# A hybrid decoder layer: the opening products on an input that has adaLN's scale but not yet its shift

## The chip, the cores and the metric

The kernel runs on one core of a Trainium2 chip. The metric is the device time of one execution in microseconds, the median of the runs. PE is TensorE (matmuls), DVE VectorE, ACT ScalarE, POOL GpSimd; SP issues the loads. Each engine works through its own instructions in order.

## The reference

One layer with hidden size D = 2048, T = 512 tokens, batch 1, all in float32:

```
mod = silu(c) @ w_ada + b_ada                  # shift, scale, gate: 2048 each
h = rms_norm(x, norm_w) * (1 + scale) + shift
proj = h @ w_in                                # aq ak av ag | q k v of DeltaNet | z | b a | mg_a mg_b
y_a = (sliding-window attention of aq, ak, av with sinks) * silu(ag) @ w_o_swa
q, k, v = silu(causal conv of width 4); q, k normalised
beta = sigmoid(b); g = -exp(a_log) * softplus(a + dt_bias)
o = gated delta rule over chunks of 64         # needs the inverse of a 64x64 triangle per head and chunk
y_b = (rms_norm(o) * silu(z)) @ w_o_dn
y = sigmoid(mg_a) * y_a + sigmoid(mg_b) * y_b
out = x + gate * (y @ w_out)
```

There are 32 query and 4 key heads of 64 in attention, and 16 key and 32 value heads of 128 in DeltaNet. For the change it matters that `h` is linear in `shift`: h @ W = (h without shift) @ W + shift @ W, and the second term is one number per output column.

## The kernel before, in words

Activations are held transposed, channels on partitions. `h` is held as 16 slices (kt) of 128 channels x 512 tokens, each split into a high part `hh` and a low part `hl` for a product of float32 accuracy from three fast matmuls: `mm3` (L240 to L242) issues high x high, low x high and high x low. Weights come as raw blocks of up to 1 MB (`load_job`, issued on SP, two buffers) and are split by half blocks: ACT casts `whi` (L52), DVE subtracts to `wlo` (L53); three such halves are held. `plan` lists the blocks in the order of use. `weight_tick` issues the next split and the next load when a half has been used up.

`channel_tile` makes 128 output channels: 16 kt x 3 matmuls into one of two PSUM buffers (`pmm`). After every second kt it calls `pump`, so there are eight pumps to a tile. `pump` advances everything else: `live` generators (each says how many pumps until its next step), `slow` ones with a budget per pump (`paced`), and `side` queues with a rate (`beside`). So a tile of products is also the cover for the small work of earlier tiles. `drain_live` and `drain_slow` issue what is left of such work at once. A scheduler that plans with costs orders the instructions of each engine when the program is built.

The stages in order:

- **startup.** x is normalised and transposed (`xnT`). For each kt, adaLN's scale and shift of 128 channels are the sums over k of silu(c) times 1 MB of weights each; `load_ada` loads both. A sum is one DVE instruction over 128x2048 (L414, with an accumulator). Every second shift sum is made by PE instead, 16 small matmuls (L405) and one (L411). `adaln` turns them into `sh` (L423, L427), then ACT makes h32 = xnT * scale + shift (L432) and `hh` (L433), and `low` makes `hl` (L437, DVE). Seven products are made per kt as soon as its slice is there: v0, v1 (attention's values), ba (64 columns for beta and g), and the first four DeltaNet keys k0 to k3. They fill seven PSUM banks at once.
- **DeltaNet, mixed stage.** gates (beta, g), keys k4 to k15, the merge gates `mb` of branch B and the first of `ma` of branch A. mb0 to mb2 come first, then the keys with mb3 to mb15 mixed in, then ma0 to ma2. `merge_gate` evicts a tile with tanh (L263) and stores it for later. In the same stage runs the first of two solves (`solve`, 16 key heads in two groups) on DVE: elimination steps on `A` (L757, L764), and at its end copies of `A` into `atmp` on ACT (L769), stored to `ta_d`, and four products with beta (L777). `s0` is its entry in `slow`: budget 0.82 per pump, 1.2 from mb13 on. After ma2, `drain_live` and `drain_slow(s0)`.
- **heads.** For each of the 16 key heads the tiles q, v, v, z, z with the delta rule in between. The second solve runs beside the first eight. The convolution of a tile is an ACT step that reads the PSUM bank (L576, `yq` for queries) and three DVE steps that read it too (L580). Then ma3, ma4.
- **branch_b.** 16 + 16 tiles of output product over o (od), with ma5, ma6 ahead of the first half and ma7, ma8 ahead of the second; adaLN's `gate` runs in `side`.
- **attention.** two key tiles, 16 query and 16 gate tiles, and then ma9 to ma15. `attend` makes scores, exponentials (L1232), transposed probabilities (pP, copied at L1250), outputs `O` and `ao` (L1266), stored to `ao_d`.
- **finish.** `ao` is loaded again and split (L52, L53), output products os0 to os15, the merge with the stored gates, and the last product.

Of the kernel before, what the change touches and what calls it, by code (L numbers as in the profile page):

```python
# [7 lines left out]
F32 = mybir.dt.float32  # L8
# [3 lines left out]
ALU = mybir.AluOpType  # L12
# [19 lines left out]
NST = 4  # L32
NFIRST = 3
STW = 320 + NST * P


class Layer:
# [110 lines left out]
    def mixed(self):  # L148

        order = [("k", g) for g in range(NST, 8)]  # L150
        mb = iter(range(NFIRST, KT))
        for g in range(8, KH):
            order.append(("k", g))
            order += [("mb", next(mb)) for _ in range(1 + g % 2)]
        return order + [("mb", j) for j in mb]


    def plan(self):
# [3 lines left out]
        for j in range(NFIRST):  # L162
            wi(f"mb{j}", 96 + j)
        for kind, j in self.mixed():
            wi(f"{kind}{j}", (16 if kind == "k" else 96) + j)
        ma = lambda r: [wi(f"ma{j}", 146 + j) for j in r]
        ma(range(0, 3))
# [6 lines left out]
        ma(range(3, 5))  # L174
        for half in range(2):
            ma(range(5 + 2 * half, 7 + 2 * half))
            jobs += [(f"od{half}_{j}", a["w_od"][half, j]) for j in range(KT)]
# [7 lines left out]
        ma(range(9, 16))  # L185
# [91 lines left out]
    def build(self):  # L277
        tc, nc, a = self.tc, self.nc, self.a
        with ExitStack() as es:
# [4 lines left out]
            self.v_d = self.dram.tile([2, P, T], F32, name="v_d")  # L284
            self.hpool = es.enter_context(tc.tile_pool(name="h", bufs=1))
# [14 lines left out]
            self.mb_d = self.dram.tile([KT, P, T], F32, name="mb_d")  # L300
# [41 lines left out]
    def startup(self, st):  # L342
# [4 lines left out]
        s2 = st.enter_context(tc.tile_pool(name="st2", bufs=2, reuse_waits="tile"))  # L347
        pa = st.enter_context(tc.tile_pool(name="st_acc", bufs=1, space=PSUM, reuse_waits="tile"))
        acc, loads = {}, {}

        def load_ada(kt):
            for j in range(2):
                wa = s2.tile([P, D], F32, tag="wa", name="wa", bufs=6)
                nc.sync.dma_start(out=wa, in_=a["w_ada_ss"][kt, j])
                loads[kt, j] = wa
# [39 lines left out]
        ada = pa.tile([P, T], F32, name="ada")  # L395

        def ada_sums(kt):


            t = acc[kt] = s2.tile([P, 2], F32, tag="acc", name="acc")  # L400
            if kt % 2 == 0:
                w = loads[kt, 0].rearrange("p (k n) -> p k n", k=KT)
# [9 lines left out]
            for j in (1, 0)[: 1 + kt % 2]:  # L412
                wa = loads[kt, j]
                nc.vector.scalar_tensor_tensor(  # L414
                    out=wa, in0=wa, scalar=1.0, in1=scb, op0=ALU.mult, op1=ALU.mult, accum_out=t[:, j : j + 1]
                )
                yield

        def adaln(kt):

            t = acc[kt]
            sh = s2.tile([P, 2], F32, tag="sh", name="sh")
            nc.vector.tensor_scalar(  # L423
                out=sh[:, 0:1], in0=t[:, 0:1] if kt % 2 else ada[:, P : P + 1], scalar1=self.b_ada[:, kt : kt + 1],
                scalar2=None, op0=ALU.add,
            )
            nc.vector.tensor_scalar(  # L427
                out=sh[:, 1:2], in0=t[:, 1:2], scalar1=self.norm_w[:, kt : kt + 1], scalar2=bn[:, kt : kt + 1],
                op0=ALU.mult, op1=ALU.add,
            )  # L430
            h32 = s2.tile([P, T], F32, tag="h32", name="h32")
            nc.scalar.activation(h32, xnT[:, kt, :], AF.Identity, scale=sh[:, 1:2], bias=sh[:, 0:1])  # L432
# [9 lines left out]
        for tb in range(NTB):  # L442
# [8 lines left out]
            for q in range(4):  # L451
                i = n % 7
                ps = pa.tile([P, 4, P], F32, tag=f"x{i}", name="xtp") if i < 3 else self.psc.tile([P, 4, P], F32, tag="sc", name="xtp")
# [7 lines left out]
                n += 1  # L461

        def products(kt, parts):
            f, l = kt == 0, kt == KT - 1
# [1103 lines left out]
```

## Time and profile before

| | us |
|---|---|
| median of 3 runs | 2930.38 (2930.1 to 2932.3) |
| span of the profiled execution (the time from its first to its last instruction) | 2929.7 |
| PE busy in it | 2870.6 |
| DVE, ACT, POOL busy | 1787.2, 1085.1, 243.0 |

The profiled execution has no time of its own other than its span; the span lies 0.7 us under the median of the runs and 0.4 under the fastest. A row of a group has the line, the engine, the operation, what it writes and reads, the shape and how often; then its busy time, the mean of one in ns, and the idle time just before it with what ended that. A row of a timeline has start, duration, and in brackets the idle time before it. The times of matmuls overlap, since they are pipelined: their starts tell the pace.

### The profile page before, as it was taken

What the parts mean: (1) busy time and instruction counts of PE and PEld (TensorE: products, weight loads), DVE (VectorE), ACT (ScalarE), POOL (GpSimd) and SP (SyncE); (2) the same over time, 40 slices, a digit from 0 to 9 for tenths busy, and PEclk for the clock granted to TensorE, in tenths of its full rate; (3) what the DMA queues carried; (4) which work ended last, traced back from release to release, by engine and by line L of the source; (5) the groups of instructions that cost most, each with busy time, mean ns of one, the idle gap of its engine ahead of it and who ended that gap; (6) DMA issues with size and microseconds to landing.
All of it is one profiled execution on the core that took longest, in us unless ns stands there. A gap on an engine that the chain in (4) does not pass through costs nothing.

```text
span 2929.7 us, 38073 instructions
## 1 busy us (share of the span) xinstructions
PE 2870.6 (98%) x14556; PEld 2351.2 (80%) x14556; DVE 1787.2 (61%) x2915; ACT 1085.1 (37%) x2113; POOL 243.0 (8%) x204
## 2 busy tenths in 40 slices
PE   8899999999999999999999999999999999999988
PEld 6677888888888888888888788888787877888867
DVE  6775998777776545544444553434655655553697
ACT  4355333333334333333333322212343443432343
POOL 0022211100000110000000000000100000000022
PEclk9999999999999999999999999999999999999999
DMA  9747555633334533333332675554322223375562
GB/s 387 281 147 219 163 169 159 203 109 111 125 113 134 160 116 124 115 122 109 123 109 100 235 263 182 186 172 141 105 89 94 85 89 103 119 262 172 173 194 97
DMA packets 175046, 451.11 MB, mean 154 GB/s; under 512 B 72433, under 2 KB 74993, under 8 KB 138897
## 3 DMA queue, kind: packets, MB, share of 16 engines
q1 hardware_dynamic: 174866, 448.70, 46.1%
q8 instruction: 114, 1.87, 0.3%
q14 instruction: 66, 0.54, 0.1%
HBM read 386.95 MB, written 59.45 MB: 152 GB/s over the span
## 4 chain that ended last, share of the span: by engine, by line
PE 84%; DVE 3%; DMA 2%; issue 1%; ACT 1%; POOL 1%; SPq 0%; POOLq 0%; DVEq 0%; ACTq 0%
PE mm L240 24%; PE mm L242 24%; PE mm L241 24%; DVE wlo L53 1%; PE S L1208 1%; PE pv L918 1%; PE po L937 1%; PE O L1259 1%; PE pP L274 1%; PE po L936 1%; PE pd L933 1%; PE pp L908 1%; PE m L241 1%; PE m L242 1%; PE m L240 1%
## 5 line engine op out<-in xcount | busy, mean ns | idle before, releaser
L240 PE MATMUL mm<-hh,whi 128*128 128x512 f32 x2784 | 1130.7, 406 | 2.3 <-ACT whi L52 1.6
L242 PE MATMUL mm<-hh,wlo 128*128 128x512 f32 x2784 | 1089.6, 391 | 1.3 <-DVE wlo L53 1.3
L241 PE MATMUL mm<-hl,whi 128*128 128x512 f32 x2784 | 1087.3, 391 | 0.0
L53 DVE TENSOR_TENSOR wlo<-raw,whi 128x1024 fp32r<-128x1024 f32 (+1 forms) x452 | 554.4, 1229 | 491.5 <-ACT whi L52 481.7
L52 ACT CAST whi<-raw 128x1024 fp32r<-128x1024 f32 (+1 forms) x452 | 470.7, 1044 | 972.9 <-PE mm L241 927.3
L242 PEld LDWEIGHTS mm<-hh,wlo 128*128 128x128 f32 x2784 | 522.6, 188 | 115.1 <-DVE wlo L53 2.2
L240 PEld LDWEIGHTS mm<-hh,whi 128*128 128x128 f32 x2784 | 523.7, 188 | 112.3 <-issue 8.4
L241 PEld LDWEIGHTS mm<-hl,whi 128*128 128x128 f32 x2784 | 524.2, 188 | 98.7 <-issue 0.4
L240 PE MATMUL mm<-oh,whi 128*128 128x512 f32 x512 | 200.6, 393 | 2.6 <-ACT oh L52 1.7
L242 PE MATMUL mm<-oh,wlo 128*128 128x512 f32 x512 | 199.4, 390 | 0.5 <-DVE wlo L53 0.5
L241 PE MATMUL mm<-ol,whi 128*128 128x512 f32 x512 | 199.5, 390 | 0.1
L865 POOL TENSOR_TENSOR qe<-qe,yq 128x512 f32<-128x512 f32 x32 | 51.4, 1624 | 902.7 <-DMA qe<-eg_rows 836.9
L714 POOL TENSOR_TENSOR E<-E,neg_g 128x512 f32<-128x512 f32 x64 | 78.4, 1224 | 476.2 <-DMA E<-g_rows 342.8
L240 PEld LDWEIGHTS mm<-oh,whi 128*128 128x128 f32 x512 | 96.0, 188 | 24.8 <-ACT oh L52 3.0
L241 PEld LDWEIGHTS mm<-ol,whi 128*128 128x128 f32 x512 | 96.1, 188 | 22.2 <-DVE ol L53 1.3
L764 DVE TENSOR_TENSOR A<-A,atmp 128x62 f32<-128x62 f32 (+30 forms) x124 | 112.9, 911 | 1.5
L242 PEld LDWEIGHTS mm<-oh,wlo 128*128 128x128 f32 x512 | 96.1, 188 | 20.9 <-DVE wlo L53 1.3
L757 DVE TENSOR_TENSOR atmp<-A 128x62 f32<-128x62 f32 (+30 forms) x124 | 109.3, 882 | 1.5
L911 DVE SCALAR_TENSOR_TENSOR r<-pp,neg_eg,vt 128x128 f32<-128x128 f32 x96 | 29.2, 346 | 78.8 <-PE pp L908 77.6
L1232 ACT ACTIVATE sm<-sm,mx,rs 128x256 f32<-128x256 f32 (+1 forms) x128 | 71.7, 561 | 3.3 <-DVE mx L1227 3.3
L580 DVE SCALAR_TENSOR_TENSOR yv<-mm,convh,yv 128x511 f32<-128x511 f32 (+2 forms) x96 | 71.5, 745 | 1.6
L241 PE MATMUL m<-wlo,hh 128*128 128x512 f32 x128 | 51.8, 404 | 10.1 <-DVE wlo L53 10.1
(331 smaller groups left out, 3145.6 us busy)
## 6 DMA issues: line engine op xcount, KB each, us to landing
raw<-in_w_ch SPq DMA_DIRECT2D x158, 1024.0 KB
wa<-in_w_ada_ss SPq DMA_DIRECT2D x32, 1024.0 KB
raw<-in_w_od SPq DMA_DIRECT2D x32, 1024.0 KB
E<-g_rows SPq DMA_DIRECT2D x64, 256.0 KB
gw<-in_w_ada_gate SPq DMA_DIRECT2D x16, 1024.0 KB
raw<-in_w_os SPq DMA_DIRECT2D x16, 1024.0 KB
qe<-eg_rows SPq DMA_DIRECT2D x32, 256.0 KB
o_d<-zh SPq DMA_DIRECT2D x32, 256.0 KB
```

Of the source, the lines that this page charges most:

```text
L52: self.nc.scalar.copy(out=hi, in_=src)
L53: self.nc.vector.tensor_tensor(out=lo, in0=src, in1=hi.bitcast(F32), op=ALU.subtract)
L240: nc.tensor.matmul(ps, lhsT=wh, rhs=xh, start=first, stop=False)
L241: nc.tensor.matmul(ps, lhsT=wh, rhs=xl, start=False, stop=False)
L242: self.last_mm = nc.tensor.matmul(ps, lhsT=wl, rhs=xh, start=False, stop=last).ins
L274: self.nc.tensor.transpose(dst[:, c * P : (c + 1) * P], src_cols(c), self.ident)
L580: nc.vector.scalar_tensor_tensor(out=y[:, s:], in0=ps[:, : T - s], scalar=w[:, j : j + 1], in1=y[:, s:], op0=ALU.mult, op1=ALU.add)
L714: nc.gpsimd.tensor_tensor(out=E, in0=E, in1=ng, op=ALU.add)
L757: eng.tensor_tensor(out=t, in0=A[:, m : m + 1, m + 1 :].to_broadcast([P, m, n]), in1=A[:, :m, m : m + 1].to_broadcast([P, m, n]), op=ALU.mult,
L764: eng.tensor_tensor(out=A[:, :m, m + 1 :], in0=A[:, :m, m + 1 :], in1=t, op=ALU.add)
L865: nc.gpsimd.tensor_tensor(out=qf, in0=qf, in1=q, op=ALU.mult)
L1232: nc.scalar.activation(t, t, AF.Exp, scale=r[:, h : h + 1], bias=mx[:, h : h + 1], accum_out=den[:, h : h + 1])
```

## The change

In the startup the input gets only the scale (`high(kt, False)`). The sums for the scale come first (16, one per kt, two of them on PE), then those for the shift (16). The products per kt are v0, v1 and mb0 to mb4, stored as they are, without tanh, to `v_d` and `mb_d`. Then mb5, mb6 and mb7 follow as ordinary tiles on the same input, with twelve shift sums between their steps, also stored raw. After them, `high(kt, True)` makes the slices again with the shift, and one pass over the 16 kt makes ba and k0 (weights `w_tr`). All tiles after that see the full input.

Keys k1 to k15 are tiles of the mixed stage, and mb8 to mb15 and ma0 to ma5 lie among and behind them; the first solve's budget goes to 1.2 at ma2. ma6 and ma7 follow the heads, ma8 to ma11 lie in branch B, ma12 to ma15 follow attention. For the ten tiles without shift (v0, v1, mb0 to mb7), `shift_products` makes shift @ W in branch B: a second load of these weights, a multiply on POOL, a reduction on DVE, a one-column matmul; the results become `bias_v` and `bias_h`. They are added where the stored tiles are read: an ACT step on v0 and v1 in attention, an ACT tanh with bias on mb0 to mb7 in the second half of branch B. The number of large products is the same.

The diff, cut to its core:

```diff
-NST = 4
-NFIRST = 3
-STW = 320 + NST * P
+NST = 5
+NPRE = 8
+STW = (2 + NST) * P
+TRW = 2 * VH + P
+NMA = 6
+FROM_PE = (0, 1)
...
     def mixed(self):
-        order = [("k", g) for g in range(NST, 8)]
-        mb = iter(range(NFIRST, KT))
-        for g in range(8, KH):
+        fill = iter([("mb", j) for j in range(NPRE, KT)] + [("ma", j) for j in range(NMA)])
+        order = []
+        for g in range(1, KH):
             order.append(("k", g))
-            order += [("mb", next(mb)) for _ in range(1 + g % 2)]
-        return order + [("mb", j) for j in mb]
+            if g >= 8:
+                order += [next(fill) for _ in range(1 + g % 2)]
+        return order + list(fill)
...
+        def high(kt, shifted):
             h32 = s2.tile([P, T], F32, tag="h32", name="h32")
-            nc.scalar.activation(h32, xnT[:, kt, :], AF.Identity, scale=sh[:, 1:2], bias=sh[:, 0:1])
+            if shifted:
+                nc.scalar.activation(
+                    h32, xnT[:, kt, :], AF.Identity, scale=scale[:, kt : kt + 1], bias=self.shift[:, kt : kt + 1]
+                )
+            else:
+                nc.scalar.activation(h32, xnT[:, kt, :], AF.Copy, scale=scale[:, kt : kt + 1])
             nc.scalar.copy(out=self.hh[:, kt, :], in_=h32)
             return h32
...
+        for i in range(3, 7):
+            load_ada(i)
+        nxt = high(0, False)
+        ada_sum(1)
+        low(0, nxt)
...
         for kt in range(KT):
+            nxt = kt + 1 < KT and high(kt + 1, False)
+            load_ada(kt + 7)
+            if kt + 2 < KT:
+                ada_sum(kt + 2)
             if kt + 1 < KT:
                 low(kt + 1, nxt)
+            wh, wl = self.half(f"st{kt // 2}")
...
             self.half_done()
             self.weight_tick()
+            if kt >= KT - 2:
+                ada_sum(2 * kt - KT + 4)
+                ada_sum(2 * kt - KT + 5)
...
+        def shifts():
+            for i in range(4, KT):
+                ada_sum(KT + i)
+                load_ada(KT + i + 6)
+                yield 2
...
+        self.go(shifts(), 1)
+        for j in range(NST, NPRE):
+            store(self.channel_tile(f"mb{j}"), self.mb_d[j])
+        self.drain_live()
+        ba = pa.tile([2 * VH, T], F32, tag="x2", name="ba")
+        self.acc_k = self.psc.tile([P, T], F32, tag="sc", name="k0")
+        low(0, high(0, True))
+        for kt in range(KT):
+            nxt = kt + 1 < KT and high(kt + 1, True)
+            if kt % 4 == 0:
+                wh, wl = self.half(f"tr{kt // 8}")
+            if kt + 1 < KT:
+                low(kt + 1, nxt)
+            x, o = (self.hh[:, kt, :], self.hl[:, kt, :]), kt % 4 * TRW
+            for ps, o, w in ((ba, o, 2 * VH), (self.acc_k, o + 2 * VH, P)):
+                self.mm3(ps, (wh[:, o : o + w], wl[:, o : o + w]), x, kt == 0, kt == KT - 1)
...
-                        self.merge_gate("mb", j, self.mb_d)
-                        if j == KT - 3:
+                        self.merge_gate("ma", j, self.ma_d)
+                        if j == 2:
                             s0[1] = 1.2
...
-            self.beside(self.gate(wk, pg), 0.2, "gate")
+            self.beside(self.shift_products(wk, pg), 0.3, "gate")
+            self.beside(self.gate(wk, pg), 0.3, "gate")
...
+                        if j < NPRE:
+                            nc.scalar.activation(th, th, AF.Tanh, scale=0.5, bias=self.bias_h[:, j : j + 1])
...
+                nc.scalar.activation(t, t, AF.Identity, bias=self.bias_v[:, i : i + 1])
...
-            for j in range(9, KT):
+            for j in range(NMA + 6, KT):
                 self.merge_gate("ma", j, self.ma_d)
...
+    def shift_products(self, wk, pp):
+        nc, a = self.nc, self.a
+        st = a["w_st"].rearrange("u p (b c) -> p u b c", b=2)
+        src = [st[:, :, :, i * P : (i + 1) * P] for i in range(2 + NST)] + [a["w_ch"][96 + j] for j in range(NST, NPRE)]
+        ps = pp.tile([P, T], F32, tag="g", name="pshift")
+        for n, w_d in enumerate(src):
+            w = wk.tile([P, D], F32, tag="gw", name="sw", bufs=1)
+            if n < 2 + NST:
+                wb = w.rearrange("p (u b c) -> p u b c", b=2, c=P)
+                for b in range(2):
+                    nc.sync.dma_start(out=wb[:, :, b, :], in_=w_d[:, :, b, :])
+            else:
+                nc.sync.dma_start(out=w, in_=w_d)
+            yield
+            wv = w.rearrange("p (k c) -> p k c", c=P)
+            nc.gpsimd.tensor_tensor(
+                out=wv, in0=wv, in1=self.shift.unsqueeze(2).to_broadcast([P, KT, P]), op=ALU.mult
+            )
+            yield
+            r = wk.tile([P, P], F32, tag="sr", name="sr", bufs=1)
+            nc.vector.tensor_reduce(out=r, in_=w.rearrange("p (k c) -> p c k", c=P), axis=AX.X, op=ALU.add)
+            yield
+            nc.tensor.matmul(ps[:, n : n + 1], lhsT=r, rhs=self.ones[:, 0:1], start=True, stop=True)
+        self.bias_v = self.const.tile([P, 2], F32, name="bias_v")
...
```

153 lines of the change are left out of this document (80 added, 73 removed).

## The prediction

> **What bounds the kernel now.** I read the page first, then the table of windows, then the groups and waits of the opening. The page says that TensorE (PE) is nearly always busy.
>
> ```profile
> span 2929.7 us, 38073 instructions
> PE 2870.6 (98%) x14556; PEld 2351.2 (80%) x14556; DVE 1787.2 (61%) x2915; ACT 1085.1 (37%) x2113; POOL 243.0 (8%) x204
> ```
>
> 2929.7 − 2870.6 leaves 59 us in which PE does nothing, and the change adds and removes no large product. So it can win only where PE idles or runs at a low clock, and it loses where it opens a new hole. The windows (columns: length, busy us and instructions of each engine, granted clock, DMA share, GB/s) show where the holes are:
>
> ```profile
> core 0: us, PE busy (x) PEld busy (x) DVE busy (x) ACT busy (x) POOL busy (x), PEclk, DMA share, GB/s
> 31.05:142.39 111.34, 96.10 (x574) 70.99 (x575) 84.88 (x111) 35.40 (x55) 0.00 (x0) 0.94 0.85 327
> 142.39:197.10 54.71, 52.94 (x256) 42.89 (x255) 34.28 (x65) 26.38 (x61) 8.52 (x8) 1.00 0.47 155
> 524.00:600.00 76.00, 76.00 (x384) 62.99 (x383) 61.90 (x89) 27.73 (x52) 11.79 (x10) 1.00 0.59 182
> 2500.00:2700.00 200.00, 199.25 (x983) 163.55 (x982) 99.67 (x160) 69.73 (x116) 0.00 (x0) 1.00 0.54 188
> ```
>
> 31.05 is the first opening product, 142.39 the first matmul of tile mb0. The second row holds 240 matmuls of 128x512 (mb0 to mb4) and a few small ones: 54.71 / 240 = 0.228 us each when nothing is in the way. At that pace the 16 × 21 = 336 opening products need 76.6 us; they take 111.3. About 35 us is all that the opening has to give. The last two rows, the start of the heads and the end of attention, are full: PE idles 0.00 and 0.75 us.
>
> What the opening waits for stands in its groups (VectorE, then ScalarE; mean ns of one behind the comma) and in PE's waits:
>
> ```profile
> L414 DVE SCALAR_TENSOR_TENSOR wa<-wa,silu_cb 128x2048 f32<-128x2048 f32 x23 | 52.5, 2283 | 0.0
> L53 DVE TENSOR_TENSOR wlo<-raw,whi 128x832 fp32r<-128x832 f32 x14 | 14.3, 1022 | 6.5 <-ACT whi L52 6.5
> L437 DVE TENSOR_TENSOR hl<-h,hh 128x512 fp32r<-128x512 f32 x16 | 11.0, 689 | 12.2 <-ACT hh L433 12.2
> L427 DVE TENSOR_SCALAR sh<-acc,norm_wT,bn 128x1 f32<-128x1 f32 x15 | 4.1, 272 | 0.5
> ...
> L432 ACT ACTIVATE h<-xnT,sh 128x512 f32<-128x512 f32 x15 | 12.2, 814 | 64.0 <-DVE sh L427 64.0
> L52 ACT CAST whi<-raw 128x832 fp32r<-128x832 f32 x13 | 11.4, 881 | 6.5 <-PE k L241 6.5
> L433 ACT CAST hh<-h 128x512 fp32r<-128x512 f32 x15 | 9.2, 616 | 0.3
> ...
> PE v L240 <- ACT hh L433: 17.3, 13, 3.3
> ```
>
> PE waits 17.3 us for `hh`; ACT waits 64.0 us for `sh`; and DVE, which makes `sh`, is busy 84.88 of 111.34 us, 52.5 of it in L414. One and a half sums per kt, a split and a `hl` make the step. Each wait also costs clock:
>
> ```profile
> 135.24 0.73 PE L240 MATMUL v<-hh,whi 128*128 128x512 f32 x2 [3.33 <-ACT hh L433]
> ...
> 139.16 0.63 PE L240 MATMUL k<-hh,whi 128*128 128x512 f32 x1
> 139.59 0.63 PE L241 MATMUL k<-hl,whi 128*128 128x512 f32 x1
> ...
> 140.33 0.40 PE L240 MATMUL k<-hh,whi 128*128 128x512 f32 x1
> 140.56 0.39 PE L241 MATMUL k<-hl,whi 128*128 128x512 f32 x1
> ```
>
> After an idle of 3.33 us matmuls start 0.43 us apart, and 0.23 apart again from 140.33 on: some 10 of them lose 0.2 us, 2 us for one long hole. The Trainium skill ("TensorE: Matmul & The Clock Gate", Part 1) says that an idle window of about 3.4 us halves the clock until a busy one has passed. By that each hole would cost 1.7 us, an estimate from its figure, and three of them 5 us where I take 6: the trace agrees, and short waits stay free by both.
>
> **Part 1, the opening: gain.** The step now needs only the scale half: one sum per kt (14 on DVE, 2 on PE), and the 16 shift sums follow, 4 beside the last steps and 12 beside mb5 to mb7. Per kt DVE has 2.28 + 0.08 (readout) + 0.27 + 0.69 + 1.1 (split of 896 columns, scaled from 1.02 at 832) = 4.45 us, PE 21 × 0.228 = 4.79. So PE becomes the bound, narrowly. The first sum goes to PE, which takes one L414 and one L427 out of the lead-in: products start at 31.05 − 2.6 = 28.4.
>
> One hole stays. The load of the third startup weight (st2) stands on SP's queue behind the loads of scale sums 3 to 8, and in DVE's order its first split stands behind all those sums. From the start on DVE therefore does a split 1.1, seven sums with their small steps 7 × (2.36 + 0.3) = 18.6, seven `hl` 4.8, another split 1.1, constants 0.5, and the split in question 1.1: 27.2, with handoffs 28, so it is ready at 56.4. PE wants it at 28.4 + 4 × 4.79 = 47.6: a hole of 8.8, and 2 of clock. From there 12 × 4.79 = 57.5 end the loop at 116; mb5, mb6, mb7 are 144 × 0.228 = 32.8, to 149. DVE's own work from 56 on is 23 sums (63), 8 `hl` (6) and 20 splits (22), 91 us, to 147: it just keeps up.
>
> Then the pass with the shift: 96 matmuls, 21.9 us, but ACT makes h and hh again, 16 × (0.81 + 0.62) = 22.9, with four weight casts of 0.8 to 1.05 between, 27 us: ACT is the bound, and it begins some 2 us after mb7, for the first `hl`. End at 178. That is 336 + 144 + 96 = 576 matmuls; before, the 336 + 240 end at 197.1. **Gain 19 us** (14 if DVE falls behind by 5, 28 if the hole at the fifth step isn't there). DMA isn't the bound: x with 4 MB, adaLN with 32, the startup weights with 7 and the next ones with 5 make 48 MB by 149 us, 320 GB/s, and the row above has 327.
>
> **Part 2, the mixed stage into the heads: loss.** The first solve starts at pump 108 of 256 instead of 85 of 248 (a pump is two kt of a tile), and has 124 pumps at 0.82 and 24 at 1.2 = 130 of budget instead of 123 × 0.82 + 40 × 1.2 = 149. It is not done when q0 comes, and `drain_slow` issues the rest at once: four pairs of `atmp` copies on ACT and four products by beta on DVE, now inside q0 and v0. Before, the copies were at:
>
> ```profile
> 515.16 2.17 ACT L769 COPY atmp<-A 64x512 f32<-64x512 f32 x2
> ...
> 522.54 2.14 ACT L769 COPY atmp<-A 64x512 f32<-64x512 f32 x2 [1.84 <-DMA ta_d<-atmp]
> ...
> 536.93 0.68 ACT L576 ACTIVATE yq<-mm,convh 128x512 f32<-128x512 f32 x1
> ```
>
> A pair waits for the stores of the one ahead: 7.4 us a pair. ACT works in order, and in the new order the eviction `yq` of q0 stands behind all of them and behind a weight cast that needs the buffer which v0 gives back at its end. PE's queue then holds v1, whose first matmul needs q0's PSUM bank (there are two), and everything behind it. So after v0's last matmul come a cast, its subtract, three steps of the second solve and five convolution steps:
>
> ```profile
> L53 DVE TENSOR_TENSOR wlo<-raw,whi 128x1024 fp32r<-128x1024 f32 (+1 forms) x452 | 554.4, 1229 | 491.5 <-ACT whi L52 481.7 <-PE pqk L869 5.7 <-PE pgate L1483 3.7
> L764 DVE TENSOR_TENSOR A<-A,atmp 128x62 f32<-128x62 f32 (+30 forms) x124 | 112.9, 911 | 1.5
> L757 DVE TENSOR_TENSOR atmp<-A 128x62 f32<-128x62 f32 (+30 forms) x124 | 109.3, 882 | 1.5
> L580 DVE SCALAR_TENSOR_TENSOR yv<-mm,convh,yv 128x511 f32<-128x511 f32 (+2 forms) x96 | 71.5, 745 | 1.6
> ```
>
> 1.05 + 1.23 + 3 × 0.9 + 5 × 0.745 = 8.7 us idle, 1.5 more at the transposes of q0 that wait for the same chain, 2 of clock: **loss 12 us** (4 if the chip's queues hand q0 over earlier than the order suggests, 18 if the copies end after v0).
>
> **Part 3, the end of attention: loss.** ma12 to ma15 instead of ma9 to ma15 follow the last attention tiles, and the last `attend` needs 16 pumps (two tiles) more than they give. Those steps are drained ahead of the output products, which use what they make:
>
> ```profile
> 2548.97 0.60 ACT L1232 ACTIVATE sm<-sm,mx,rs 128x256 f32<-128x256 f32 x1
> ...
> 2557.98 0.59 ACT L1250 COPY pT<-pP 128x512 f32<-128x512 f32 x1
> ...
> 2567.13 4.72 ACT L52 CAST hh<-aoraw 128x512 fp32r<-128x512 f32 x7 [1.43 <-PE mm L242]
> ```
>
> From the exponentials to the first reads of `ao` were 18 us, spread over two tiles. With no tiles left, only output products of kt 0 to 11 (os0, os1: 72 matmuls, 16 us) lie beside them. I count 1 us for the PSUM of the scores, 2.6 for the transposes of P, and 4 until the last four channels have gone out, come back and been split: 7.6, and 1 of clock. **Loss 8.6 us** (0.75 as before, if the order overlaps it fully; 14 if nothing of the last 18 us but the 72 matmuls hides).
>
> **Part 4, the shift products: little.** Ten loads of 1 MB, ten multiplies on POOL, ten reductions on DVE, ten one-column matmuls, all beside the tiles of branch B. The nearest POOL row:
>
> ```profile
> L865 POOL TENSOR_TENSOR qe<-qe,yq 128x512 f32<-128x512 f32 x32 | 51.4, 1624 | 902.7 <-DMA qe<-eg_rows 836.9 <-DVE osb L968 60.9 <-DMA tt<-ts_d 4.9
> ```
>
> Four times its size is 6.5 us, 65 in all, on an engine that is 8% busy over the span. A reduction reads as much as L414 does: 2.3 us, 23 in all. At 0.3 steps per pump a product takes three steps, ten pumps or 13.7 us (48 × 0.228 = 10.9 for the eight pumps of a tile), so both fit, and a split that waits for one of them still has two halves of weights (10.9 us) ahead of it. The loads (17 issues on SP) are as far apart. The matmuls and their drains: +1.5 us (0 to 5). The ten extra tanh and bias steps lie on ACT, which is a third busy. Nothing on PE pays for the second scale (`gate` at 0.3): it ends before it is used.
>
> **Sum.** −19 + 12 + 8.6 + 1.5 = +3 on the span of 2929.7: 2932.7. The median of the runs, 2930.4, is 0.7 above the span: 2933. About 0.2%, 6 us, is what a measurement of this kernel can tell from no change; +3 is inside it.
>
> **Rivals.** *Faster: the new holes are shallow.* The orders of ACT and DVE were read from the built program, but which wait binds depends on arrivals. If q0's bank comes free halfway (6 instead of 12) and attention costs 3, the sum is −19 + 6 + 3 + 1.5 = −8.5, 2922; without the hole at the fifth step as well, 2912. For it: the trace of before shows PE full at both places, with the same steps squeezed into few tiles. Against: there, each had tiles as cover that are moved now.
>
> *Slower: the late first solve.* If DVE finishes the elimination later than 1 us after q0's start, the four pairs (3 × 7.4 + 2.1 = 24 us, begun in ma5) end after v0, and each further microsecond goes to PE: at 6 late, loss 18 in part 2. With the opening's gain cut to 17 by DVE's narrow margin: −17 + 18 + 8.6 + 1.5 = +11, 2941. For it: DVE has 4.45 against 4.79 in the loop and is 62 of 76 us busy at the heads. Against: before, the last pair began at 522.54, ahead of q0, and there are only 19 units of budget less.
>
> *A smaller gain in the opening.* The 30 sums on DVE are still 71 us, and all must be done before the pass with the shift. If handoffs stretch DVE's 91 us by a tenth to 100, it ends at 156 instead of 147, the opening at 156 + 2 + 27 = 185, the gain is 12 and the sum +10, 2940. Against: the shift sums lie beside tiles that need only 0.2 of DVE.
>
> **Chances.** As summed, within 6 us: 0.30. Shallow holes, or no hole at the fifth step: 0.34 faster. Late solve, or the opening short of its gain, or attention dearer: 0.36 slower. The forecast is 2933; its own range is 2926 to 2940. The range over the cases is 2912 to 2946: the lower end is the faster rival with both its parts, the upper the late solve with attention at 14.
>
> **What would show it.** Right: first product near 28.4, a wait of `mm3` for `wlo` at the fifth step of some 9 us; k1 near 178; PE idle 8 to 10 us at v1, with `yq` far behind q0's end; PE idle 6 to 9 us around os0. Wrong in part 1, if the wait for `hh` is still above 5 us; in part 2, if PE stays full from q0 to v1; in part 3, if it stays full from ma15 to os1; in part 4, if branch B's PE idles more than 5 us.

## The result, and the profile after

The changed kernel takes 2971.39 us (median of 4 runs, 2969.02 to 2972.25), the kernel before 2931.34 beside it: 1.0133 times as long, with a 95% interval of 1.0121 to 1.0145. The forecast was 2933. The page of the profiled execution has:

```profile
span 2967.2 us, 37825 instructions
## 1 busy us (share of the span) xinstructions
PE 2881.7 (97%) x14372; PEld 2360.7 (80%) x14372; DVE 1864.2 (63%) x2955; ACT 1111.4 (37%) x2149; POOL 270.1 (9%) x214
```

The starts of the tiles in the timelines of PE (the first matmul of each) cut both spans into stages. Where tiles were moved from one stage to another, 48 × 0.2267 = 10.88 us per tile is taken off:

| stage | before | after | tiles moved | change |
|---|---|---|---|---|
| start to q0 | 525.1 | 542.1 | +3 | −15.6 |
| q0 to q1 | 60.7 | 79.2 | 0 | +18.4 |
| q1 to the end of z31 | 1012.1 | 1012.6 | 0 | +0.5 |
| to the first attention tile (branch B and the ma tiles ahead of it) | 429.8 | 451.5 | 0 | +21.7 |
| attention to the end of ag15 | 454.2 | 456.0 | 0 | +1.8 |
| to os2 (the end of attention) | 118.0 | 95.5 | −3 | +10.1 |
| os2 to the end | 329.7 | 330.3 | 0 | +0.6 |

The changes add up to 37.5 us, the difference of the spans. What PE waits for over the whole span (total, how often, longest) names most of the places:

```profile
PE m L244 <- DVE wlo L56: 10.2, 6, 5.4
PE mm L243 <- DVE yq L627: 9.1, 1, 9.1
PE ptkT L277 <- ACT k L712: 8.1, 6, 2.7
PE mm L244 <- DVE ol L56: 7.0, 4, 4.2
PE ptq L277 <- DVE yq L634: 6.2, 1, 6.2
PE v L243 <- ACT whi L55: 5.2, 1, 5.2
PE pshift L1534 <- DVE sr L1532: 4.3, 3, 2.5
PE mm L243 <- ACT hh L55: 3.9, 1, 3.9
```

`yq` and `ptq` lie between q0 and z0, `ol` and `pshift` in branch B, `v` at the fifth step of the opening, the last row at os1. The windows of these places (opening, pass with the shift, mixed stage, q0 to q1, od0_0 to od0_2) show idle PE and a clock below 1 together, except in the mixed stage:

```profile
core 0: us, PE busy (x) PEld busy (x) DVE busy (x) ACT busy (x) POOL busy (x), PEclk, DMA share, GB/s
28.40:117.29 88.89, 82.88 (x387) 67.39 (x386) 75.77 (x96) 37.78 (x54) 0.00 (x0) 0.96 0.89 351
150.00:172.75 22.75, 17.85 (x68) 10.86 (x67) 13.88 (x19) 19.61 (x30) 0.00 (x0) 0.92 0.37 129
300.00:500.00 200.00, 197.76 (x930) 163.69 (x929) 172.88 (x251) 77.97 (x168) 43.00 (x32) 1.00 0.55 169
542.12:621.28 79.16, 63.85 (x309) 51.81 (x308) 52.28 (x76) 30.61 (x48) 10.48 (x10) 0.89 0.56 171
1686.44:1738.98 52.54, 41.16 (x152) 31.00 (x150) 28.62 (x20) 14.28 (x20) 14.94 (x4) 0.87 0.66 217
```

Before, the tiles od0_0 to od0_2 and the stretch from q0 to q1 had been:

```profile
1648.65:1686.85 38.20, 34.95 (x146) 26.21 (x144) 21.48 (x19) 13.69 (x20) 0.00 (x0) 1.00 0.80 283
525.12:585.83 60.71, 60.71 (x309) 50.07 (x308) 52.00 (x72) 21.70 (x40) 11.79 (x10) 1.00 0.68 209
```

In branch B the first three output tiles took 17.6, 16.6 and 18.3 us instead of 12.1, 13.1 and 13.1. The timeline of DVE there:

```profile
1690.94 4.09 DVE L56 TENSOR_TENSOR ol<-oraw,oh 128x512 fp32r<-128x512 f32 x1
1694.96 3.69 DVE L1532 TENSOR_REDUCE sr<-sw 128x128 f32<-128x2048 f32 x1
```

and that of POOL:

```profile
1690.80 3.69 POOL L1527 TENSOR_TENSOR sw<-sw,shift 128x2048 f32<-128x2048 f32 x1 [12.81 <-DMA sw<-in_w_st]
```

A subtract for `ol`, otherwise 0.69 us, takes 4.09, until POOL's multiply has ended; behind it stands a reduction of 3.69. So the next slice of o is 7 us later. SP's waits for the subtract that gives a slice's buffer back are hardly longer than before (18.3 us from 1655 to 1745; 16.8 from 1619 to 1707 before). New on that queue, with the loads of o behind them, are five waits, 22.9 us in all, of a load of shift weights for the reduction that gives back its one buffer. PE waits 7.0 us for `ol` and 4.3 for `sr` in branch B, where before it waited 3.1 us in all, for `oh` and weights.

The hand-over from the mixed stage to the heads, in the timeline of ACT:

```profile
558.41 1.05 ACT L55 CAST whi<-raw 128x1024 fp32r<-128x1024 f32 x1 [2.31 <-PE mm L244]
560.14 2.17 ACT L813 COPY atmp<-A 64x512 f32<-64x512 f32 x2 [0.68 <-DMA ta_d<-atmp]
563.85 1.04 ACT L55 CAST whi<-raw 128x1024 fp32r<-128x1024 f32 x1 [1.54 <-PE mm L244]
564.80 0.68 ACT L623 ACTIVATE yq<-mm,convh 128x512 f32<-128x512 f32 x1
565.38 0.68 ACT L623 ACTIVATE yv<-mm,convh 128x512 f32<-128x512 f32 x1
578.59 0.63 ACT L903 ACTIVATE E<-E 128x512 f32<-128x512 f32 x1 [12.53 <-POOL E L759]
579.12 0.61 ACT L632 ACTIVATE th<-yq 128x512 f32<-128x512 f32 x1
```

in that of DVE (between these two rows stand a subtract for weights and four steps of the second solve):

```profile
562.35 4.63 DVE L821 TENSOR_TENSOR A<-A,bet 128x1024 f32<-128x1024 f32 x4 [0.66 <-ACT atmp L813]
569.65 0.74 DVE L627 SCALAR_TENSOR_TENSOR yq<-mm,convh,yq 128x511 f32<-128x511 f32 x1
```

in that of SP's queue:

```profile
564.74 5.17 SPq L828 DMA_DIRECT2D ts_d<-A  x4
570.01 3.45 SPq L751 DMA_DIRECT2D E<-g_rows  x2
```

and in that of PE:

```profile
573.16 0.76 PE L243 MATMUL mm<-hh,whi 128*128 128x512 f32 x1 [9.12 <-DVE yq L627]
580.97 1.09 PE L277 MATMUL ptq<-ident,yq 128*128 128x128 f32 x4 [6.18 <-DVE yq L634]
```

q0 ended at 553.0; its eviction `yq` comes at 564.80, behind the last copies and a cast that waits for v0's end. Its convolution on DVE, which v1's buffer needs, begins at 569.65, behind the four products by beta and the steps after them. That is the first wait. The second has another way: SP stores `ts_d` only when the products by beta are done, the loads of E for the first head stand behind these stores (570.01), POOL and ACT then make E (578.59), and `th`, which q0 needs, stands behind E on ACT.

### The profile page after: what moved, and what is told of

Same layout as the page of the kernel before. It is cut to its first block, busy times and chain, and to the rows that moved or that the text cites. A ratio compares the mean times of both kernels' runs of the same rounds, so it can differ in the third digit from the quotient of the medians.

```text
span 2967.2 us, 37825 instructions
## 1 busy us (share of the span) xinstructions
PE 2881.7 (97%) x14372; PEld 2360.7 (80%) x14372; DVE 1864.2 (63%) x2955; ACT 1111.4 (37%) x2149; POOL 270.1 (9%) x214
## 4 chain that ended last, share of the span: by engine, by line
PE 79%; DVE 6%; DMA 4%; issue 2%; ACT 1%; POOL 1%; SPq 0%; POOLq 0%; DVEq 0%; ACTq 0%
PE mm L243 23%; PE mm L245 22%; PE mm L244 22%; DVE wlo L56 2%; DMA oraw<-o_d 1%; PE S L1256 1%; PE pv L962 1%; PE po L981 1%; PE O L1307 1%; PE pP L277 1%; PE po L980 1%; PE pd L977 1%; PE pp L952 1%; PE m L244 1%; ACT whi L55 1%
## 5 line engine op out<-in xcount | busy, mean ns | idle before, releaser
L56 DVE TENSOR_TENSOR wlo<-raw,whi 128x1024 fp32r<-128x1024 f32 (+2 forms) x452 | 565.7, 1254 | 451.6 <-ACT whi L55 446.8
L55 ACT CAST whi<-raw 128x1024 fp32r<-128x1024 f32 (+2 forms) x452 | 470.5, 1043 | 937.7 <-PE mm L244 869.7
L243 PEld LDWEIGHTS mm<-hh,whi 128*128 128x128 f32 x2752 | 519.8, 189 | 122.2 <-issue 17.6
L422 DVE SCALAR_TENSOR_TENSOR wa<-wa,silu_cb 128x2048 f32<-128x2048 f32 x30 | 68.4, 2284 | 0.0
```

Of the source, the lines that this page charges most:

```text
L55: self.nc.scalar.copy(out=hi, in_=src)
L56: self.nc.vector.tensor_tensor(out=lo, in0=src, in1=hi.bitcast(F32), op=ALU.subtract)
L243: nc.tensor.matmul(ps, lhsT=wh, rhs=xh, start=first, stop=False)
L422: nc.vector.scalar_tensor_tensor(out=wa, in0=wa, scalar=1.0, in1=scb, op0=ALU.mult, op1=ALU.mult, accum_out=acc)
```

## The experiments

All runs are set against the kernel before on the same chip; "stage" is a stage of the table above. Theories of the first round: the excess of branch B comes from SP's queue; the holes behind q0 from the drained end of the first solve; that of attention from the missing cover.

**Shift products later** (program order alone).

```diff
-self.beside(self.shift_products(wk, pg), 0.3, "gate")
+self.beside(self.shift_products(wk, pg), 0.4, "gate")
+        for _ in range(16):
+            yield          # at the head of shift_products
```

> The changed kernel, but the shift products of branch B start 16 steps (40 pumps, five tiles) later, behind the loads of the first half of o, and go at 0.4 steps per pump. Theory A (SP's queue: a load of shift weights waits at the head of SP for its one buffer, which the reduction gives back, and the loads of o stand behind it): od0_0 to od0_2 fall back to the lengths of before (about 12, 13, 13 us instead of 17.6, 16.6, 18.3), about 14 us less in all, 2957. Rival B (the multiply on POOL and the reduction on DVE, 3.6 and 3.7 us each, cost PE's weights their split wherever they run): the loss moves to later tiles and the time stays within 4 us of 2971.

2980.5 us. The stage of branch B takes 462.7 instead of 451.5. The edit did not do what it says: SP issued the first shift load at 1667.6, as early as without it (1667.4), since nothing tied it to its place. It decides nothing on the queue.

**Shift loads on POOL's queue.**

```diff
-                    nc.sync.dma_start(out=wb[:, :, b, :], in_=w_d[:, :, b, :])
+                    nc.gpsimd.dma_start(out=wb[:, :, b, :], in_=w_d[:, :, b, :])
```

(and the same for the contiguous loads)

> The changed kernel, with the loads of the shift weights issued from POOL's queue instead of SP's; their place and the arithmetic stay. Theory A (SP's queue): the loads of o no longer stand behind a wait for the shift buffer, od0_0 to od0_2 lose most of their excess, 10 to 15 us less, 2958. Rival B (POOL and DVE work itself, or the traffic of the extra loads): no more than 4 us less, 2967 to 2975.

2980.07 us; branch B 461.3, with od0_0 at 26.4. SP was free of these loads and the price stayed, so a wait on SP does not make it alone. On POOL the loads stood in a queue with the multiplies, which may have had a price of its own; the rest of the excess has to be looked for on DVE and PE.

**A faster first solve.**

```diff
-s0 = self.paced(self.solve(sol0, 0, nc.vector), 0.82)
+s0 = self.paced(self.solve(sol0, 0, nc.vector), 1.0)
```

> The changed kernel, with the first solve's budget 1.0 per pump instead of 0.82 until ma2. It then has 124 + 29 = 153 units before q0, where it needed about 149. Theory A (the holes at v1 and at q0's transposes come from the drained end of the first solve): q0 to q1 falls from 79 to 61 us, 18 less, 2953. Rival B (DVE is the limit in the mixed stage: 298 of 369 us busy): the work only moves, splits of weights come late between the keys, and no more than 8 us are won, 2963 or above.

2976.51 us. q0 to q1 falls to 68.6, but q0 starts at 557.7 instead of 542.1. What PE waited for:

```profile
PE ptkT L277 <- ACT k L712: 11.2, 6, 2.8
PE ptk L277 <- DVE y L634: 1.4, 1, 1.4
```

and the window from 300 to 500 us, columns as above:

```profile
300.00:500.00 200.00, 188.60 (x863) 154.27 (x863) 175.48 (x247) 73.20 (x159) 38.91 (x28) 0.98 0.50 157
```

DVE is little busier than in the changed kernel (172.88), and PE does 9 us less. The rival's number holds: nothing is won. That more of the solve now stands ahead of the steps of the keys on DVE is the likely reason, read from these rows and not tested by itself.

**The kernel before with the new places of ma** (six, two, four, four instead of three, two, four, seven; the loops that compute the tiles are changed alike).

```diff
-ma(range(0, 3)) ... ma(range(3, 5)) ... ma(range(5 + 2 * half, 7 + 2 * half)) ... ma(range(9, 16))
+ma(range(0, 6)) ... ma(range(6, 8)) ... ma(range(8 + 2 * half, 10 + 2 * half)) ... ma(range(12, 16))
```

> The kernel before, with nothing of the change but the places of the ma tiles: six in the mixed stage, two behind the heads, four in branch B, four behind attention (before 3, 2, 4, 7). Theory A (the last attend needs 16 pumps more than four tiles give): ma15, os0 and os1 get longer as in the changed kernel, 12 us more than before, 2943. Rival B (that loss comes from something else of the change, such as the added steps on v): within 3 us of before, 2928 to 2934.

2952.18 us, ratio 1.0062. From the end of ag15 to os2 it loses 10.7 us against before, as the changed kernel does (10.1): the loss at the end of attention comes from the missing tiles alone. PE there waits 4.5 us for `hh`, and 1.7 for the scores, and the clock is 0.94. Not expected: q0 to q1 is 69.6, 8.9 more than before, though the first solve was done. There ACT has E ahead of `yq`, and E comes late (573.86 and 575.59, then `yq` at 577.06, in v0, which began at 568.5).

**No shift products** (their loads, multiplies, reductions and matmuls left out; one small matmul fills the buffer that is read later).

```diff
-for n, w_d in enumerate(src):
+nc.tensor.matmul(ps[:, 0:16], lhsT=self.ones, rhs=self.ones[:, 0:16], start=True, stop=True)
+for n, w_d in enumerate(src[:0]):
```

> The changed kernel without the shift products: their loads, multiplies, reductions and matmuls are left out, and the ten tiles get a constant in place of shift @ W. Everything else keeps its place; adaLN's gate then starts at once, as in the kernel before, at 0.3. Theory A (the whole excess of branch B comes from the shift products): from ma6 to the first attention tile 20 us less, 2951. Rival B (the excess comes from the different places of ma tiles, or of gate's loads, which start earlier here): at most 8 us less, 2963.

2946.38 us. Branch B takes 429.2 us, 429.8 before: the shift products cost the whole 22 us.

**Four buffers for the slices of o.**

```diff
-raw = wk.tile([P, T], F32, tag="oraw", name="oraw")
+raw = wk.tile([P, T], F32, tag="oraw", name="oraw", bufs=4)
```

> The changed kernel with four buffers instead of two for the slices of o that branch B loads. Theory A (the loads of o are a chain of latencies over two buffers: load, cast on ACT, subtract on DVE, buffer back, next load; a multiply on POOL that keeps DVE waiting 3.6 us, or a reduction of 3.7 us in front of a subtract, lengthens each turn): with four buffers the turns overlap, and ma6 to od0_3 loses at least 10 of its 16 us, 2960. Rival B (PE waits for the splits of weights behind the same steps, not for o): no more than 4 us less.

2967.01 us. Up to od0_3 8.7 us are won, a little less than theory A asks, and 8.6 are lost in the rest of the first half (od0_7 takes 18.3); the second half is 4.0 shorter. Shortening one chain moved much of the price to where it met others. The stage is 447.3.

**Copies at the end of the solve on POOL.** At L813:

```diff
-            nc.scalar.copy(
+            nc.gpsimd.tensor_copy(
```

> The changed kernel with the copies of A into atmp at the end of each solve made by POOL instead of ACT. Theory A (first hole at v1: the eviction of q0 stands on ACT behind copies and a cast that waits for v0's end): the 9.1 us at v1 go; the wait of q0's transposes (6.2 us) stays, since the store of A to ts_d on SP still stands ahead of the loads of E. About 9 us less, 2962. Rival B (DVE is late by itself at the end of the solve): the wait at v1 stays above 5 us.

2971.88 us, and v1 waits 10.3. On ACT:

```profile
560.42 1.04 ACT L55 CAST whi<-raw 128x1024 fp32r<-128x1024 f32 x1 [4.38 <-PE mm L244]
561.37 0.68 ACT L623 ACTIVATE yq<-mm,convh 128x512 f32<-128x512 f32 x1
```

Without the copies `yq` still stands behind the cast that waits for v0's end, and DVE has the four products by beta (560.06 to 564.69) ahead of its steps; these had waited for the last copy, now POOL's. So the copies' place on ACT was not what held q0. What their end costs by way of the products, this run doesn't tell.

**Shift products later and tied.** As the first, with each step tied behind the last large matmul.

```diff
-                if next(q[0][0], True):
+                with self.behind():
+                    done = next(q[0][0], True)
+                if done:
```

> As the kernel with the later shift products, but each step of them is tied behind the last large matmul at its place, since without that the first loads were issued at the start of the loads of o all the same. Theory A (shift products only hurt beside the loads of o): od0_0 to od0_2 as before (12, 13, 13 us), and later tiles 11 us: from ma6 to the first attention tile 14 us less than in the changed kernel, 2957. Rival B (they cost wherever they run): less than 5 us less.

2985.86 us. od0_0 to od0_2 take 11.1, 11.2 and 11.0 us, better than before, and od0_4 to od0_12 take 12 to 18. The wait there:

```profile
PE pshift L1538 <- DVE sr L1536: 19.8, 8, 4.1
```

PE works in order: a one-column matmul held its queue until load, multiply and reduction had gone through one buffer, 14 us, where the rate gave them ten.

**The first solve finished before q0** (eight ma tiles in the mixed stage, none behind the heads).

```diff
-NMA = 6
+NMA = 8
-ma(range(NMA, NMA + 2)) ... ma(range(NMA + 2 + 2 * half, NMA + 4 + 2 * half)) ... ma(range(NMA + 6, KT))
+ma(range(8, 8)) ... ma(range(*((8, 10), (10, 12))[half])) ... ma(range(12, KT))
```

> The changed kernel with ma6 and ma7 moved from behind the heads into the mixed stage: eight, none, four, four. The first solve gets 16 more pumps, 19 units, before q0. Theory A (both holes between q0 and v1 come from the end of the first solve, issued at once): they go, q0 to q1 falls from 79 to 61 to 65 us, and if the end of the heads hides without the two tiles the kernel is 15 us faster, 2956. Rival B (they come from the order in which the eviction of q0 and the loads of E are put there, whatever is left of the solve): q0 to q1 stays above 70, as in the kernel before with six ma tiles moved there (69.6). The last heads without cover could cost 10 by both.

2959.14 us. In the window from q0 to q1 nothing is left of the holes:

```profile
561.61:622.31 60.70, 60.70 (x309) 50.04 (x308) 50.04 (x71) 21.80 (x40) 12.91 (x10) 1.00 0.65 206
```

60.7 us as before: the last copies begin at 557.63, ahead of q0's start at 561.64, and not 18 us behind it. A finished solve isn't enough by itself, though: in the kernel before with the new places of ma it was done too, and 8.9 us were lost there, by its trace to E standing ahead of `yq`. The end of the heads without its two tiles takes 16 us more (z31 29.4 instead of 13.1).

**Tied, slower, matmul one step later.** Start after 12 / 0.3 = 40 pumps, each step tied as before, and the matmul of product n − 1 comes after the load of product n; two buffers for `sr`.

```diff
+        for _ in range(12):
+            yield
 ...
+            if last:
+                nc.tensor.matmul(ps[:, n - 1 : n], lhsT=last, rhs=self.ones[:, 0:1], start=True, stop=True)
-            r = wk.tile([P, P], F32, tag="sr", name="sr", bufs=1)
+            r = wk.tile([P, P], F32, tag="sr", name="sr", bufs=2)
```

> The changed kernel, with each step of the shift products tied to its place as in the held kernel, started 40 pumps after the start of branch B at 0.3 steps per pump (the held one had 0.4), and each one-column matmul issued only after the next product's load, so that PE has a third of a tile more before it needs the reduction. Theory A (PE was held by these matmuls: 19.8 us in the held kernel, since load, multiply, reduction take 14 us over one buffer and had 10): od0_0 to od0_2 stay at 11 us, and the tiles after them at 11: from ma6 to the first attention tile 22 us less than in the changed kernel, 2948. Rival B (POOL and DVE keep the weights' splits): tiles beside them stay above 12 us, less than 8 us won.

2960.52 us; branch B 441.6, 10 less than the changed kernel, half of what was expected. od0_11 (17.2) and od1_0 (16.2) still meet a product.

**st2 earlier.**

```diff
-        for i in range(3, 7):
-            load_ada(i)
+        load_ada(3)
+        load_ada(4)
+        self.split_half()
+        self.weight_tick()
+        load_ada(5)
+        load_ada(6)
```

> The changed kernel with the second startup weight split earlier and the third one's load (st2) issued ahead of the loads of scale sums 5 and 6. Theory A (the hole at the fifth step is st2's place on SP and behind the sums on DVE): the 5.2 us wait goes with its slow clock, mb5 starts at 110 instead of 117 and q0 7 us earlier, if nothing later takes it back; 2964. Rival B (DVE sets the opening's end: 30 sums before the pass): mb5 starts earlier, but the pass with the shift begins when it did, 2970.

2967.04 us. The wait at the fifth step is 1.9 instead of 5.2 us, mb5 starts at 111.2, and q0 at 537.3. In two other runs of that round q0 started at 539.4 and 539.8 without it, so some 2 us are kept. The four last kernels below have this order too, with eight ma tiles ahead of q0: it starts at 558.1 to 561.4 there, and at 561.6 in the kernel with eight tiles and the old order. So little of the 4 us at mb5 reaches q0.

**Six tiles behind attention, none behind the heads.**

```diff
-ma(range(NMA, NMA + 2)) ... ma(range(NMA + 2 + 2 * half, NMA + 4 + 2 * half)) ... ma(range(NMA + 6, KT))
+ma(range(6, 6)) ... ma(range(*((6, 8), (8, 10))[half])) ... ma(range(10, KT))
```

> The changed kernel with ma6 and ma7 moved from behind the heads to the end: six, none, four, six. Theory A (the end of attention lacks two tiles): the excess from ag15 to os2, 30 us, falls to 20 as before, 10 us less, minus what the last heads lose without cover; 2961 if they lose nothing. Rival B: the heads' end loses as much as attention wins, 2971.

2971.56 us. The end of attention wins 8 us, the end of the heads loses 14 (z31 27.1). The sixteen ma tiles are cover at four places, and taking them from one shows there.

**Shift products beside the second half of the heads**, 0.14 steps per pump, tied, reductions stored, ten matmuls together in branch B.

```diff
-self.beside(self.shift_products(wk, pg), 0.3, "gate")
+self.beside(self.shift_products(wk), 0.14, "shift")    # in the second half of the heads
+self.shift_sums(wk, pg)                                # in branch B: load and ten matmuls
 ...
-nc.tensor.matmul(ps[:, n : n + 1], lhsT=r, rhs=self.ones[:, 0:1], start=True, stop=True)
+nc.sync.dma_start(out=self.sr_d[n], in_=r)
```

> The changed kernel with the shift products beside the second half of the heads (0.14 steps per pump, tied to their places, reductions stored, and the ten one-column matmuls together at the start of branch B). Theory A (they cost by their place): the heads stay at 1012.6 us from q1 to the end of z31, branch B falls by 18 or more to what it was without them (429 us for its 36 tiles and the two ahead), 2949. Rival B (a multiply on POOL and a reduction on DVE of 3.6 us each delay whatever runs beside them): the heads get 10 us or more longer, and the time stays above 2959.

2956.19 us: between the theories. Branch B is at 432.0, 3 us above what it is without them; the heads, where PE had no wait before, lose 11.2 us. PE waits for `ptv`, `pu` and `pd`, the steps of a head that come through DVE. So the price is one of place and of work: it is smaller here, and it doesn't go away.

**All of it at once.** The kernel above, st2 earlier, ma at eight, two, one and one, four; four buffers for o; `gate` held back.

> As the kernel with the shift products in the heads, and with it the earlier load of st2, the ma tiles at eight, two, one and one, four, four buffers for the loads of o, and adaLN's gate held back by 40 pumps. Theory A (the losses are separate and each is undone): opening 17 to 20 us better than before, q0 to q1 as before, heads as before, branch B within 4, the end of attention 10 worse: 2923, faster than both. Rival B (one tile ahead of each half of branch B doesn't hide the loads of o, and the heads pay for the shift products): 10 to 15 us back, 2935, no better than before.

2939.51 us, ratio 1.0028 (1.0020 to 1.0037). q0 to q1 is 60.7, but the heads lose 11, the end of attention 11.

**Its two single tiles behind attention too** (eight, two, none and none, six).

```diff
-MAB = ((10, 11), (11, 12))
+MAB = ((10, 10), (10, 10))
```

> The same with no ma tile in branch B and six behind attention. Theory A (four buffers let the slices of o arrive fast enough for four PSUM banks): branch B loses no more than 8 us against two tiles of cover, and the end of attention is as before: 2923, as with four tiles. Rival B (each half of branch B waits for its first slices): 20 us lost there, 2940.

2941.07 us, the same within their spread. The end of attention is 2.6 from before; ma9, ahead of od0_0, takes 26.8 us.

**Small pieces.** Each multiply and each reduction in four pieces, at 0.34 steps per pump, and the ten matmuls ahead of od0_3.

```diff
-nc.gpsimd.tensor_tensor(out=wv, ...)
+for c in range(4):
+    k4 = slice(4 * c, 4 * c + 4)
+    nc.gpsimd.tensor_tensor(out=wv[:, k4], ...)
+    yield
```

> As the kernel with six ma tiles behind attention, with each multiply and each reduction of the shift products in four pieces of about 0.9 us (0.34 steps per pump), and the ten one-column matmuls ahead of od0_3 instead of at the start of branch B. Theory A (the price is the length of single steps ahead of others in their queues, and the wait of the matmuls for their load): the heads fall from 1023 to within 3 us of 1012, the tile before od0_0 from 26.8 to 13, and the time to 2914 to 2920, faster than the kernel before. Rival B (the work itself): the heads stay above 1020, 2925 or more.

2934.58 us. The heads fall from 1023.0 to 1016.0, so the length of single steps is over half of that price. The matmuls didn't keep their place: PE had them at 1674.4, in ma9, three tiles early, and waited there for their load:

```profile
PE pshift L1563 <- DMA gs<-sr_d: 6.9, 1, 6.9
```

**The ten matmuls tied** behind the last large matmul of od0_2.

```diff
-self.shift_sums(sr, pg)
+with self.behind():
+    self.shift_sums(sr, pg)
```

> As the last kernel, with the ten one-column matmuls tied behind the last large matmul of od0_2. Theory A (they wait on PE for their load, 6.9 us, and the clock is slow after it): ma9 falls from 26.8 to 13 us, the time to 2918 to 2922, faster than the kernel before. Rival B (with no ma tile in branch B, PE waits at the same place for the first slices of o): ma9 and od0_0 together stay above 35 us, 2929 or more.

2933.01 us beside 2932.1, ratio 1.0004 (0.9995 to 1.0013): no difference. ma9 and od0_0 together are 37.8 us. The rival holds: with the matmuls at od0_2, PE waits at the same place for the slices of o, so their wait had covered another one:

```profile
PE mm L246 <- ACT oh L56: 8.8, 2, 8.2
```

No version beat the kernel before. In the last one, by the stages of the table with the moved tiles taken off, the opening and the mixed stage are 21.5 us better than before and q0 to q1 is even; branch B, four tiles short, is 14.6 worse, the heads 3.4, attention and its end 5.4, the rest 1.5. Most of what is won ahead of q0 is spent on cover.

## Why the prediction was wrong, point by point

**The opening: right.** Forecast 19 us; by the prediction's own measure, the end of 576 matmuls, it is 197.1 − 180.4 = 16.7, and 15.6 at q0. Ten profiles with this opening have q0 between 538.7 and 544.4, so one of them tells this gain to some 3 us. First products began at 30.5 instead of 28.4. The hole at the fifth step came where it was said, and is smaller: 5.2 us and slow clock for 8.8 and 2. mb5 started at 117.3 (116 forecast). The pass with the shift was the longest part left, with PE busy 17.85 of 22.75 us and ACT 19.61; since 30 of its products stand behind the first matmul of k1, it ended at 180.4 (178). Two sums of this part are slightly off, without effect: DVE's step adds up to 4.42 us, not 4.45, and its 23 sums at the step's prices to 61, not 63.

**q0 to v1: mechanism right, size short.** Forecast 12, measured 18.4. The first wait, 8.7 forecast, was 9.1. The term that failed is "1.5 more at the transposes of q0": it is 6.2, because it was read as the same chain through ACT, and is a second one through SP's stores, the loads of E, POOL and ACT. That the unfinished solve causes both is shown by the run that finishes it: 60.7 us. The argument for it in the prediction, the copies ahead of `yq` on ACT, is not: the last one ended at 562.3, ahead of v0's end at 564.0, and with the copies on POOL nothing changed. What the rows show is the order behind v0's end: the cast ahead of `yq` on ACT, and on DVE the products by beta until 567.0, a subtract, the steps of the second solve and the convolution. The prediction's 8.7 has no term for the products, which take about 3 us behind v0's end; it adds the cast, which here ran beside them, and 2.7 us for steps of the solve that took 1.7. That it came so near to 9.1 is in part luck.

**The end of attention: right in its place and cause, near in size by some luck.** Forecast 8.6, measured 10.1, and 10.7 in the kernel before with only the tiles moved. The last wait, 4 forecast, was 3.9, and that for the scores 1.6 for 1. For the transposes of P, 2.6 forecast, PE had no wait. In their place stands the clock, forecast at 1 us: from ag15's end to os2 PE idles 5.8 us (0.75 before), so about half of the loss isn't idle time, and the granted clock is 0.96 (1.00 before), 0.86 in os0.

**The shift products: wrong.** Forecast 1.5 (0 to 5), measured 22. This is the step that failed: "so both fit, and a split that waits for one of them still has two halves of weights (10.9 us) ahead of it". It counted busy time and asked after the splits of weights alone. Three queues were left out: DVE's steps for the slices of o, which od0_0 needs at once and which go through two buffers; PE, whose one-column matmuls wait for the reduction (4.3 us here, 19.8 when held); and the loads that one buffer ties to the reduction. The multiply on POOL was 3.61 us (median) for 6.5 by scaling, the reduction 3.8 for 2.3: together 7.4 us a product where 8.8 were counted, so it wasn't busy time that ran short. The prediction's own sign of being wrong here, more than 5 us of idle PE in branch B, showed: 11.4 in od0_0 to od0_2 alone. That the shift products are the cause is shown by the run without them. Which of the three queues has which part of the 22 us isn't settled: the runs moved the price from one to another.

**The sum.** −19 + 12 + 8.6 + 1.5 became −15.6 + 18.4 + 10.1 + 21.7, with 2.9 in stages that were costed at nothing. Without the shift products the kernel is 13.5 us slower than before (2946.38 beside 2932.84), where the other three terms of the sum gave +1.6: part 2 with 6.4 more than forecast, the opening with 3.4 less won, and the stages costed at nothing make up most of that. The clock terms of the sum are 2, 2 and 1 us, so 5, and not the 6 that the prediction says it took. The rival on the other side named the late solve, with 18 in part 2; 18.4 came, but by the order behind v0, not by late copies. Its 2941 lacked the shift products. The range ended at 2946 with 1.5 us for part 4; with the 5 that the prediction allowed it would have been 2950, with 21.7 it is 2967.

## What to carry to other kernels

Work that fits into an engine's idle time isn't hidden by that: ask for each new step which step stands behind it in the queue, and how soon PE needs that one. Ten products, each with a multiply and a reduction of 3.6 to 3.8 us, cost 22 us beside a chain over two buffers and 11 beside the heads; in pieces of about 1 us they cost 4 beside the heads. When tiles are the cover for other work, moving some of them earlier is paid where they were: count every place's need before taking from one. And an edit of the program's order says nothing of the engine's order as long as a scheduler is free to undo it.

## What the runs showed of the hardware that was not expected

A subtract of DVE with two SBUF inputs that began 0.14 us into a multiply of POOL took 4.09 instead of 0.69 us, ending 0.54 us after it. The Trainium skill ("SBUF — State Buffer", "SBUF: two separate sides") says that such a DVE step and a POOL step that reads SBUF share a pair of ports, which the first to start keeps for its whole instruction. The trace agrees with a full block here: 4.09 is 3.55 of waiting and 0.54 of work. A POOL multiply by a broadcast vector was also faster per element (128x2048 in 3.61 us, a piece of 128x512 in 1.04) than the two-tensor one of the same engine in the kernel before (128x512 in 1.28 at its fastest, 1.42 in the median).

The prediction took short waits to be free. Two of them in a row were not: PE waited 0.76 us, did two matmuls, and waited 2.40 more until 1715.09, and the granted clock from 1714.0 to 1717.4 was 0.66, as after the single wait of 4.18 us in od0_0 (0.65 from 1693.6 to 1697.0).
